# Queries and keys turned as float32 rows, and split behind PSUM: one core of a Trainium2 chip

## The chip, the cores and the metric

The kernel runs on one core of one Trainium2 chip. A core has TensorE (matrix products and transpositions, into PSUM), VectorE, ScalarE and GpSimd for elementwise work, and queues for transfers from HBM. The metric is the time of one execution on the device in microseconds (us), less is better. In the rows PE is TensorE's matmul, PEld its weight load, DVE VectorE, ACT ScalarE, POOL GpSimd.

## The reference

One layer of a decoder with 256 tokens and 1024 channels: two attention mixers in parallel, merged by sigmoid gates, then an MLP with squared ReLU. Cut to what matters:

```python
h = _rmsnorm(x, norm1_g[i])
proj = h @ w_in[i]
...
q_a = _rope(_rmsnorm(q_a.reshape(B, S, NSA_HEADS, dh), q_norm_a[i]), pos).reshape(B, S, G, R, dh)
k_s = _rope(_rmsnorm(k_s.reshape(B, S, G, dh), k_norm_slc[i]), pos)
k_w = _rope(_rmsnorm(k_w.reshape(B, S, G, dh), k_norm_win[i]), pos)
y_a = _nsa_mixer(q_a, k_c, v_c, k_s, v_s, k_w, v_w, g_nsa, ...)
q_b = _rope(_rmsnorm(q_b.reshape(B, S, DIL_HEADS, dh), q_norm_b[i]), pos)
k_b = _rope(_rmsnorm(k_b.reshape(B, S, DIL_HEADS, dh), k_norm_b[i]), pos)
y_b = _dilated_mixer(q_b, k_b, v_b)
mixed = jax.nn.sigmoid(g_ma) * (y_a @ w_o_a[i]) + jax.nn.sigmoid(g_mb) * (y_b @ w_o_b[i])
```

The first mixer (NSA) has 12 query heads of 64 in 3 key groups, over selected, window and compressed keys; the second (dilated) has 12 query and 12 key heads. Scores are sums of q times k over the 64 channels of a head.

## The kernel before

Products carry float32 as two float32r parts, hi = float32r(x) and lo = x - hi, and three passes (hi hi, hi lo, lo hi). Weights stream from HBM in pieces of 128x768. Of each piece ScalarE makes hi (L180), and VectorE, for some pieces GpSimd, makes lo (L183), five to eight pieces ahead of their use.

Projections (`proj`, L294 to L296) give rows: 128 tokens on the partitions, up to 420 columns, in two token tiles (t = 0, 1). In order: compressed keys and values, selected and window keys and values (3 key heads each), queries of the first mixer in two halves of 6 heads (qa0, qa1) beside the compression MLP, the first gates (L744 to L746), then for each half of the second mixer queries (dq), keys (dk) and values, 6 heads each; then the other gates and the first output projection.

Behind each projection a task works on the rows. `normrope` squares and sums per head, takes the power -0.5 on GpSimd (L315), rotates with the tables (L321 on GpSimd, L324 and L327 on VectorE) in the tile t1 (two buffers), and multiplies by the norm in place (L329). Then:

- queries (`q_out`): ScalarE copies the rows into hi (L342), VectorE makes lo = v - hi (L343), each head as 128 columns [hi, lo]. Six float32r transpositions (L335, in `turn`, three to a PSUM bank) give per head hi on partitions 0 to 63 and lo on 64 to 127; ScalarE casts three heads at a time out of PSUM (L336).
- keys (`k_out`): each head is written twice, as [hi, hi] (L353) and as [lo, lo] (L354), then transposed as two tiles (L335) and cast by ScalarE (L336). A score is then two products of a query tile, with [hi; hi] and with [lo; lo] (L552 for the first mixer, L693 for the second).
- the 48 compressed keys likewise (L457 to L469).

There are 8 query tiles (6 heads), 4 key tiles of 3 heads and 4 of 6 heads. The split rows lie in tiles with the tag "qk", four buffers. The attention tasks (`nsa`, `dil`) wait for the events that these tasks set; their probabilities are transposed as float32 (L511), cast to hi by ScalarE out of PSUM (L515), and lo is made by VectorE from PSUM (L516; for the compressed keys L644, L645).

The order of the program is made by `Order`: products are emitted in sequence, and steps of the tasks are set in between when a clock of estimated TensorE time says that they are due (`yield D["rope"]` leaves 8 us of it between the rows and their transposition, D["turn"] 0.3 us). A scheduler below orders the instructions of each engine by their priority and their estimated times. Each engine runs its queue in order. PSUM has 4 banks for accumulators and 6 for all else, transpositions among it.

## Time and profile before

| | us |
|---|---|
| median of 3 runs | 474.08 |
| lowest and highest | 473.75, 474.11 |
| span of the profiled execution | 474.4 |
| busy in it: TensorE, VectorE, ScalarE, GpSimd | 452.3, 351.9, 295.0, 209.0 |

The page gives each engine's busy time and its share of the span, the span in 40 slices, the chain of work that ended last, and the costliest groups of instructions. Matmuls are pipelined, so one's record is longer than the time that it takes from the next one: for that the chain of waits is read, whose pieces do not overlap.

### The profile page before, as it was taken

Reading aid. Unit: us, or ns where it says so; the run is one execution under the profiler, and the core shown is the slowest. Engines: PE = TensorE matmul, PEld = TensorE weight load, DVE = VectorE, ACT = ScalarE, POOL = GpSimd, SP = SyncE. Lnnn points to the kernel's source line nnn. Section 1 sums busy time; section 2 is a strip of 40 time slices with the busy share of each in tenths; the row PEclk is TensorE's granted clock in tenths of the full one; section 3 lists DMA queues with packets and bytes.
Section 4 is the critical chain, followed back from the end, with each engine's and each line's share of the span. In section 5 each row is a group of like instructions: output and inputs, shape, how many; then the busy total and the mean of one; then the engine's idle time right before and its main releaser. Section 6 shows DMA issues by size and latency. Waiting matters only on the chain.

```text
span 474.4 us, 9304 instructions
## 1 busy us (share of the span) xinstructions
PE 452.3 (95%) x3472; PEld 436.4 (92%) x3474; DVE 351.9 (74%) x572; ACT 295.0 (62%) x637; POOL 209.0 (44%) x203
## 2 busy tenths in 40 slices
PE   7997897999899999999999899999999999999996
PEld 6896777999798898989999899999999999999996
DVE  3959998989988999998557979956556555555450
ACT  5747678487867897858697454665656643433430
POOL 2797775779587782813043519523333310000000
PEclk8999899999899999999999999999999999999999
DMA  7973557563343144234336574777666767767720
GB/s 246 356 232 101 161 170 249 152 193 101 99 140 129 34 134 134 77 103 123 102 96 188 182 225 133 205 199 194 180 192 178 195 194 203 193 205 197 196 87 11
DMA packets 29630, 76.93 MB, mean 162 GB/s; under 512 B 3809, under 2 KB 5265, under 8 KB 29457
## 3 DMA queue, kind: packets, MB, share of 16 engines
q1 hardware_dynamic: 29584, 76.34, 54.5%
q8 instruction: 27, 0.44, 0.4%
q14 instruction: 19, 0.15, 0.1%
HBM read 75.28 MB, written 1.05 MB: 161 GB/s over the span
## 4 chain that ended last, share of the span: by engine, by line
PE 79%; DVE 10%; issue 4%; DMA 3%; ACT 2%; SPq 1%; POOL 0%; DVEq 0%; ACTq 0%; POOLq 0%
PE acc L745 18%; PE acc L746 18%; PE acc L744 18%; PE acc L295 4%; PE acc L296 4%; PE acc L294 4%; DVE wl L183 3%; PE tp L511 2%; DMA raw<-in_kv_c 2%; DMA gr<-in_gr 2%; PE tp L335 1%; PE dsp L693 1%; PE sp L552 1%; DVE t L329 1%; DVE h L873 1%
## 5 line engine op out<-in xcount | busy, mean ns | idle before, releaser
L183 DVE TENSOR_TENSOR wl<-raw,wh 128x768 fp32r<-128x768 f32 (+2 forms) x154 | 160.7, 1047 | 70.5 <-ACT wh L180 69.8
L180 ACT CAST wh<-raw 128x768 fp32r<-128x768 f32 (+2 forms) x183 | 152.1, 841 | 77.8 <-PE acc L745 66.2
L183 POOL TENSOR_TENSOR wl<-raw,wh 128x768 fp32r<-128x768 f32 (+1 forms) x29 | 56.2, 1937 | 62.5 <-ACT wh L180 35.8
L745 PE MATMUL acc<-h,wh 128*128 128x256 f32 x256 | 71.8, 281 | 0.7 <-DVE h L873 0.6
L745 PE MATMUL acc<-u,wh 128*128 128x256 f32 x256 | 71.6, 280 | 0.0
L746 PE MATMUL acc<-u,wl 128*128 128x256 f32 x256 | 71.6, 280 | 0.0
L744 PE MATMUL acc<-u,wh 128*128 128x256 f32 x256 | 71.6, 279 | 0.0
L746 PE MATMUL acc<-h,wl 128*128 128x256 f32 x256 | 71.3, 279 | 0.0
L744 PE MATMUL acc<-h,wh 128*128 128x256 f32 x256 | 71.3, 280 | 0.0
L295 PE MATMUL acc<-wl,hT 128*128 128x384 f32 (+1 forms) x176 | 63.0, 358 | 5.3 <-POOL wl L183 3.2
L294 PE MATMUL acc<-wh,hT 128*128 128x384 f32 (+1 forms) x176 | 60.3, 355 | 2.7 <-ACT wh L180 2.6
L296 PE MATMUL acc<-wh,hT 128*128 128x384 f32 (+1 forms) x176 | 61.1, 350 | 0.0
L911 POOL TENSOR_TENSOR r<-r 128x256 f32<-128x256 f32 x32 | 31.7, 992 | 54.1 <-ACT r L910 54.1
L745 PEld LDWEIGHTS acc<-h,wh 128*128 128x128 f32 x256 | 48.2, 188 | 1.2 <-DVE h L873 1.1
L746 PEld LDWEIGHTS acc<-u,wl 128*128 128x128 f32 x256 | 48.2, 188 | 0.0
L745 PEld LDWEIGHTS acc<-u,wh 128*128 128x128 f32 x256 | 48.2, 188 | 0.0
L744 PEld LDWEIGHTS acc<-u,wh 128*128 128x128 f32 x256 | 48.2, 188 | 0.0
L746 PEld LDWEIGHTS acc<-h,wl 128*128 128x128 f32 x256 | 48.1, 188 | 0.0
L744 PEld LDWEIGHTS acc<-h,wh 128*128 128x128 f32 x256 | 48.0, 188 | 0.0
L295 PEld LDWEIGHTS acc<-wl,hT 128*128 128x128 f32 x176 | 34.7, 197 | 7.3 <-POOL wl L183 3.7
L294 PEld LDWEIGHTS acc<-wh,hT 128*128 128x128 f32 x176 | 33.6, 194 | 4.1 <-ACT wh L180 3.5
L746 PE MATMUL acc<-hT,wl 128*128 128x256 f32 x128 | 37.0, 289 | 0.0
(195 smaller groups left out, 1094.7 us busy)
## 6 DMA issues: line engine op xcount, KB each, us to landing
raw<-in_cells SPq DMA_DIRECT2D x128, 384.0 KB, 3.4
raw<-in_cw SPq DMA_DIRECT2D x10, 384.0 KB, 3.7
raw<-in_q_a SPq DMA_DIRECT2D x8, 384.0 KB, 3.2
raw<-in_q_b SPq DMA_DIRECT2D x8, 384.0 KB, 3.6
raw<-in_k_b SPq DMA_DIRECT2D x8, 384.0 KB, 3.1
raw<-in_v_b SPq DMA_DIRECT2D x8, 384.0 KB, 3.2
raw<-in_kv_w SPq DMA_DIRECT2D x4, 420.0 KB, 8.3
raw<-in_kv_c SPq DMA_DIRECT2D x4, 384.0 KB, 7.0
```

What stands on the lines that cost most here:

```text
L180: nc.scalar.copy(hi[:, :m], src)
L183: eng.tensor_sub(lo[:, :m], src, f(hi[:, :m]))
L294: nc.tensor.matmul(o, hT[0][:, k, ts], hi[:, c], start=k == 0, stop=False)
L295: nc.tensor.matmul(o, hT[0][:, k, ts], lo[:, c], start=False, stop=False)
L296: nc.tensor.matmul(o, hT[1][:, k, ts], hi[:, c], start=False, stop=k == 7)
L329: nc.vector.tensor_mul(v, v, st[:, 1, :h][:, :, None].to_broadcast([128, h, 64]))
L335: nc.tensor.transpose(pt[:, i * 128:(i + 1) * 128], src[:, i].rearrange("p a d -> p (a d)"), idr)
L511: nc.tensor.transpose(pt[0:rows, i * 128:(i + 1) * 128], s, ident)
L744: nc.tensor.matmul(o, hi, a[0][k], start=start, stop=False)
L745: nc.tensor.matmul(o, hi, a[1][k], start=False, stop=False)
L746: nc.tensor.matmul(o, lo, a[0][k], start=False, stop=stop)
L911: nc.gpsimd.tensor_mul(r, r, r)
```

## The change

A query tile is transposed unsplit: v is float32, two heads of 64 side by side are the 128 columns of one transposition, three for six heads. As it leaves PSUM, ScalarE writes hi and VectorE lo, once for the heads on partitions 0 to 63 and once for those on 64 to 127; lo goes to the other half of the partitions, so that half of the heads are now stacked [hi; lo] and half [lo; hi]. Of a key tile L329 writes each head twice (768 columns for 6 heads); three heads are transposed as float32 at a time, ScalarE writes [hi; hi] and VectorE [lo; lo] from the same bank. The compressed keys likewise, with one transposition for two. `normrope` writes its last product into tiles of their own, "vq" and "vk", three buffers each, in place of t1; "qk" is gone, and so is the float32r identity `idr`. Shortened, the rest of the diff is removed comments:

```diff
-     "rbufs": 5, "wbufs": 5, "xb": 3, "phib": 4, "Pb": 4, "yb": 4, "sqb": 2, "t2b": 1, "t1b": 2, "qkb": 4,
+     "rbufs": 5, "wbufs": 5, "xb": 3, "phib": 4, "Pb": 4, "yb": 4, "sqb": 2, "t2b": 1, "t1b": 2, "vkb": 3, "vqb": 3,
...
-    idr = const.tile([128, 128], F32R, name="idr")
-        nc.vector.tensor_copy(idr, ident)
...
-        nc.vector.tensor_mul(v, v, st[:, 1, :h][:, :, None].to_broadcast([128, h, 64]))
-        return v
-
-    def turn(dst, src, m):
-        pt = tp_bank(F32R)
-        for i in range(m):
-            nc.tensor.transpose(pt[:, i * 128:(i + 1) * 128], src[:, i].rearrange("p a d -> p (a d)"), idr)
-        nc.scalar.copy(dst, f(pt[:, :m * 128]).rearrange("p (h c) -> p h c", c=128))
-        pe(m * 0.11)
+        if twice:
+            o = tok.tile([128, 6, 2, 64], F32, name="vk", tag="vk", bufs=D["vkb"])[:, :h]
+            nc.vector.tensor_mul(o, v[:, :, None, :].to_broadcast([128, h, 2, 64]),
+                                 st[:, 1, :h][:, :, None, None].to_broadcast([128, h, 2, 64]))
+        else:
+            o = tok.tile([128, 6, 64], F32, name="vq", tag="vq", bufs=D["vqb"])
+            nc.vector.tensor_mul(o, v, st[:, 1, :h][:, :, None].to_broadcast([128, h, 64]))
+        return o
 
     def q_out(v, t, qd):
-        ql = tok.tile([128, 6, 2, 64], F32R, name="ql", tag="qk", bufs=D["qkb"])
-        nc.scalar.copy(ql[:, :, 0], v)
-        nc.vector.tensor_sub(ql[:, :, 1], v, f(ql[:, :, 0]))
         yield D["rope"]
-        for a in range(0, 6, 3):
-            turn(qd[:, a:a + 3, t * 128:(t + 1) * 128], ql[:, a:a + 3], 3)
+        pt = tp_bank()
+        for i in range(3):
+            nc.tensor.transpose(pt[:, i * 128:(i + 1) * 128], v[:, 2 * i:2 * i + 2].rearrange("p a d -> p (a d)"), ident)
+        pe(0.35)
+        for b in range(2):
+            a, o = (slice(b * 64, b * 64 + 64), slice(64 - b * 64, 128 - b * 64))
+            src = pt[a, :384].rearrange("p (h c) -> p h c", c=128)
+            ts = slice(t * 128, (t + 1) * 128)
+            nc.scalar.copy(qd[a, b:6:2, ts], src)
+            nc.vector.tensor_sub(qd[o, b:6:2, ts], src, f(qd[a, b:6:2, ts]))
+        yield D["turn"]
+
+    def k_out(v, h, dst):
+        yield D["rope"]
+        for a in range(0, h, 3):
+            pt = tp_bank()
+            for i in range(3):
+                nc.tensor.transpose(pt[:, i * 128:(i + 1) * 128],
+                                    v[:, a + i].rearrange("p a d -> p (a d)"), ident)
+            pe(0.35)
+            src = pt[:, :384].rearrange("p (h c) -> p h c", c=128)
+            hi, lo = dst(0, a), dst(1, a)
+            nc.scalar.copy(hi, src)
+            nc.vector.tensor_sub(lo, src, f(hi))
             yield D["turn"]
-
-    def k_out(v, h, dst):
-        kd = [tok.tile([128, 6, 2, 64], F32R, name=f"kd{i}", tag="qk", bufs=D["qkb"]) for i in range(2)]
-        vb = v[:, :, None, :].to_broadcast([128, h, 2, 64])
-        nc.scalar.copy(kd[0][:, :h], vb)
-        nc.vector.tensor_sub(kd[1][:, :h], vb, f(kd[0][:, :h]))
-        yield D["rope"]
-        for i in range(2):
-            for a in range(0, h, 3):
-                turn(dst(i, a), kd[i][:, a:a + 3], 3)
-                yield D["turn"]
...
-            v = normrope(y[:, 0:192], 3, kind, t, 0.125, EPS)
+            v = normrope(y[:, 0:192], 3, kind, t, 0.125, EPS, twice=True)
...
-            v = normrope(y[:, 0:384], 6, 4, t, 0.125, EPS)
+            v = normrope(y[:, 0:384], 6, 4, t, 0.125, EPS, twice=True)
```

## Rows read from the trace of the kernel before

**Rows 1.** The page, its first part: busy us, share of the span, instructions.
```profile
PE 452.3 (95%) x3472; PEld 436.4 (92%) x3474; DVE 351.9 (74%) x572; ACT 295.0 (62%) x637; POOL 209.0 (44%) x203
```

**Rows 2.** Busy time by stretch: engines (instructions), granted clock, DMA share, GB/s.
```profile
38.00:77.00 39.00, 30.66 (x189) 26.99 (x188) 38.74 (x62) 26.72 (x57) 27.16 (x25) 0.96 0.57 169
77.00:108.00 31.00, 31.00 (x217) 30.07 (x217) 27.49 (x53) 22.83 (x63) 22.04 (x22) 1.00 0.59 180
108.00:126.00 18.00, 15.84 (x109) 14.20 (x106) 17.87 (x36) 12.99 (x36) 14.81 (x13) 1.00 0.41 117
126.00:195.00 69.00, 68.58 (x468) 63.16 (x467) 62.91 (x122) 56.20 (x171) 45.34 (x47) 0.98 0.35 108
195.00:202.00 7.00, 6.02 (x53) 5.73 (x52) 7.00 (x10) 6.19 (x13) 6.50 (x6) 1.00 0.35 92
202.00:264.00 62.00, 60.51 (x515) 58.90 (x517) 47.44 (x89) 43.36 (x93) 17.53 (x12) 1.00 0.44 135
```

**Rows 3.** Groups of instructions: count, busy us, mean ns, idle before.
```profile
L511 PE MATMUL tp<-ident,P 128*128 128x128 f32 x108 | 17.5, 275 | 0.0
...
L335 PE MATMUL tp<-idr,kd 128*128 128x128 f32 x72 | 9.1, 251 | 0.5 <-ACT kd L353 0.5
...
L335 PE MATMUL tp<-idr,ql 128*128 128x128 f32 x48 | 5.4, 250 | 0.0
```

**Rows 4.** The chain of waits near 200 us: start, us on the chain, what.
```profile
193.57 0.21 PE tp L335 x3
193.78 0.19 PE acc L745
193.96 0.12 PE acc L746
...
195.37 0.98 DVE t L324
...
203.51 0.44 PE tp L511 x4
```

**Rows 5.** The same chain at 214 us.
```profile
213.85 0.96 PE tp L335 x12
```

**Rows 6.** Single lines: count, least/median/greatest ns, first and last start in us.
```profile
L354 DVE TENSOR_TENSOR kd<-t,kd x8: 543/947/2180, 51.8 to 218.8; 128x384 fp32r<-128x384 f32 x4, 128x768 fp32r<-128x768 f32 x4
...
L329 DVE TENSOR_TENSOR t<-t,st x16: 341/600/2200, 49.5 to 204.7; 128x384 f32<-128x384 f32 x12, 128x192 f32<-128x192 f32 x4
...
L183 DVE TENSOR_TENSOR wl<-raw,wh x154: 939/958/2736, 6.7 to 460.9; 128x768 fp32r<-128x768 f32 x151, 128x840 fp32r<-128x840 f32 x2, 128x512 fp32r<-128x512 f32 x1
...
L342 ACT CAST ql<-t x8: 513/516/554, 66.5 to 196.4; 128x384 fp32r<-128x384 f32 x8
...
L294 PE MATMUL acc<-wh,hT x176: 332/337/522, 6.7 to 166.5; 128*128 128x384 f32 x160, 128*128 128x420 f32 x16
```

**Rows 7.** Groups by form, ScalarE: count, busy us, mean ns, idle before.
```profile
L336 ACT CAST dk<-tp 128x384 fp32r<-128x384 f32 x16 | 7.4, 485 | 3.4 <-PE tp L335 3.3
```

**Rows 8.** Groups by form, VectorE.
```profile
L516 DVE TENSOR_TENSOR plo<-tp,phi 128x384 fp32r<-128x384 f32 x12 | 6.2, 548 | 3.4 <-ACT phi L515 3.4
...
L343 DVE TENSOR_TENSOR ql<-t,ql 128x384 fp32r<-128x384 f32 x8 | 4.8, 596 | 0.0
L354 DVE TENSOR_TENSOR kd<-t,kd 128x768 fp32r<-128x768 f32 x4 | 4.6, 1154 | 0.0
...
L645 DVE TENSOR_TENSOR pc<-tp,pc 16x512 fp32r<-16x512 f32 x6 | 4.1, 680 | 0.2
...
L354 DVE TENSOR_TENSOR kd<-t,kd 128x384 fp32r<-128x384 f32 x4 | 3.8, 962 | 0.0
```

**Rows 9.** The chain of waits from 106 to 126 us.
```profile
117.17 0.55 DVE ql L343
...
124.49 0.69 DVE pc L645
```

**Rows 10.** TensorE in order of time: start, us, what, idle before.
```profile
125.23 0.49 PE L649 MATMUL pvo<-pc,vC 48*128 48x512 f32 x1 [2.16 <-DVE pc L645]
```

More of the change, by code (lines that the diff above doesn't have):

```diff
@@ L304, in proj, with normrope @@
                 yield 0
-    def normrope(y, h, kind, t, sumscale, eps):
+    def normrope(y, h, kind, t, sumscale, eps, twice=False):
         n = h * 64
@@ L456, in cmp_post @@
             nc.vector.tensor_add(t1[:, 0], t1[:, 0], t1[:, 1])
-            nc.vector.tensor_scalar(t1[:, 0], t1[:, 0], st[:, 1:2], None, op0=OP.mult)
-            kd = [tok.tile([48, 2, 64], F32R, name=f"kcd{j}", tag=f"kcd{j}", bufs=1) for j in range(2)]
-            vb = t1[:, 0][:, None, :].to_broadcast([48, 2, 64])
-            nc.scalar.copy(kd[0], vb)
-            nc.vector.tensor_sub(kd[1], vb, f(kd[0]))
-            yield D["ck"]
-            pt = tp_bank(F32R)
-            for j in range(2):
-                nc.tensor.transpose(pt[:, j * 48:(j + 1) * 48], kd[j].rearrange("p a d -> p (a d)"), idr[0:48, 0:48])
-            pe(0.2)
-            for j in range(2):
-                nc.scalar.copy(st_["kT"][j][:, :, 384:400],
-                               f(pt[:, j * 48:(j + 1) * 48]).rearrange("p (g c) -> p g c", g=3))
+            kd = tok.tile([48, 2, 64], F32, name="kcd", tag="kcd", bufs=1)
+            nc.vector.tensor_scalar(kd, t1[:, 0][:, None, :].to_broadcast([48, 2, 64]), st[:, 1:2], None, op0=OP.mult)
+            yield D["ck"]
+            pt = tp_bank()
+            nc.tensor.transpose(pt[:, 0:48], kd.rearrange("p a d -> p (a d)"), ident[0:48, 0:48])
+            pe(0.1)
+            src = pt[:, 0:48].rearrange("p (g c) -> p g c", g=3)
+            hi, lo = [st_["kT"][j][:, :, 384:400] for j in range(2)]
+            nc.scalar.copy(hi, src)
+            nc.vector.tensor_sub(lo, src, f(hi))
         else:
```

## The prediction

> **What bounds the kernel now.** I read the page first, then busy time by stretch, then the chain of waits inside each stretch, then single lines. The page says TensorE is busy 452.3 of 474.4 us [rows 1]; a matmul's record is longer than its share of the stream, so that is no proof. The stretches are [rows 2]. From 38 to 77 us VectorE is busy 38.74 of 39.00 us and TensorE only 30.66: VectorE sets the pace. From 77 to 108 TensorE is busy without a hole and VectorE has 3.5 us to spare. From 108 to 126 VectorE is full again (17.87 of 18.00), and TensorE has 2.16 us of idle time. From 126 to 195 TensorE leads (68.58 of 69.00), VectorE has 6.1 us free. From 195 to 202 VectorE is full (7.00 of 7.00) and TensorE loses 1 us. After 202 TensorE leads, VectorE has 14.6 us free up to 264. The last transposition that the change touches lies near 230 us, so all that follows 264 is unmoved. So one microsecond off TensorE counts from 77 to 108 and from 126 on; one microsecond on VectorE counts in 38 to 77, 108 to 126 and 195 to 202.
>
> **TensorE.** Before, a query tile takes 6 float32r transpositions and a key tile of three heads 6 (of six heads 12): 72 for keys and 48 for queries (8 query tiles of 6) [rows 3]. After, each six become three, in float32; the compressed keys go from two small ones to one and are left out of the sum. What float32 costs is seen in lines that stay: the probabilities at L511 are transposed in float32 with the same identity, 108 records for 108 transpositions [rows 3], and a run of four takes 0.44 us on the chain, 0.11 each [rows 4]. A float32r one takes 0.080 (twelve in 0.96) [rows 5]; a run of three takes 0.21, and the matmul behind it 0.19 in place of 0.12, so 0.28 for three, 0.093 each [rows 4]. Six old ones cost 0.48 to 0.56 us, three new ones 0.33: 0.15 to 0.23 us saved per six. There are 20 sixes; the four of the first keys run in the VectorE-bound stretch, 16 behind 77 us. 16 x 0.15 to 0.23 is 2.4 to 3.7 us; I take 2.9.
> [...]
>
> **ScalarE.** Per query tile: one copy of 0.516 goes [rows 6]; two casts out of PSUM stay two (half the partitions, same columns, 0.485 [rows 7]). Per key tile of three heads a cast of about 0.52 and one PSUM cast go; of six heads a cast of 768 columns (at most 2 x 0.516) and two PSUM casts. 8 x 0.52 + 4 x 1.0 + 4 x 2.0 = at most 16 us less, some 15, spread from 50 to 230. ScalarE is nowhere full [rows 2], so this is worth only what sits in a chain; it is not counted but as cover below.
>
> **VectorE.** Removed: 8 subtractions of queries (mean 0.596), 4 of three-head keys (0.962), 4 of six-head keys (1.154) [rows 8]: 4.8 + 3.8 + 4.6 = 13.2 us. Added: two subtractions from PSUM per query tile, one per three-head and two per six-head key tile: 16 + 4 + 8 = 28. The nearest row is L516 with 128x384 from PSUM, 0.548 [rows 8]; a half-height one is no cheaper, since L645 takes 0.680 with 16 partitions for 512 columns [rows 8]. 28 x 0.548 = 15.3 us. The multiplication L329 writes keys twice: 384 in place of 192 columns (0.54 for 0.34, the least of L354 and L329 [rows 6]), and 768 in place of 384 (0.94, the least of L183, for 0.54 [rows 6]): 4 x 0.20 + 4 x 0.40 = 2.4. Net +4.5 us, the one large price of the change. By stretch:
> 38 to 77: gone are the three-head L354 (3.8) and two L343 (1.2); new are 0.8 of wider multiplications and four subtractions (2.2). Net -2.0. Of this 1.6 is one L354 that took 2.180 where 0.543 is the least [rows 6]; whatever held it may hold another instruction. Bounds -2.0 and -0.4, and as the pace is VectorE's, the time follows. I take 0.8 us saved.
> 77 to 108: four new subtractions (2.2) of the first queries, less two old ones: +1.0 within 3.5 us of idle time. Nothing, as long as no product waits for them (first rival).
> 108 to 126: four new ones (2.2) and two wider multiplications (0.8), less two L343 (1.2): +1.8 on a full engine. On this chain lie L343 (0.55) and, before a 2.16 us hole of TensorE, the subtraction L645 (0.69) [rows 9, 10]. ScalarE's relief shortens the same chain by the two query copies of 0.52 that lie in it (L342 [rows 6]). Bounds: +1.8 and -1.0; I take their sum, 0.8 us lost.
> 126 to 264: eight query and eight key subtractions (8.8) and 0.8 of wider multiplication against the four six-head L354 (4.6) and two L343 (1.2): +3.8 in 20 us of idle time. Nothing by itself, and one thing better. The rotated rows now leave the t1 tile (2 buffers) at L329, where before they held it until the split had been made. The last projection product is at 166.5, yet L329 runs until 204.7 and the query split until 196.4 [rows 6]: the last key tiles' rotation comes as a burst (L324 at 195.37 [rows 4]) that fills VectorE from 195 to 202. With 3 buffers for queries and 3 for doubled keys it can start earlier. Worth 0 to 1.0 us (the TensorE time lost there [rows 2]); I take 0.6.
>
> Why L354 took 0.543 once and 2.180 another time is told by no row. [...]
>
> **Sum.** -2.9 -0.8 +0.8 -0.6 = -3.5 us. The profiled span is 474.4, the median 474.08 with runs from 473.75 to 474.11, so span and median are taken as one: 474.1 - 3.5 = **470.6 us**. About 0.2%, 0.95 us, is what a measurement of this kernel can tell from no change.
>
> **Rivals.**
> First, slower: the low part becomes a wait of TensorE. Before, both parts were made some 8 us of TensorE work ahead of the transpositions, and behind them only a cast stood. Now the low part is made behind transposition and cast, in VectorE's queue, and the scores' products L552 and L693 are issued soon after in TensorE's queue, with the projections behind them. If VectorE runs late there, TensorE stands still. And where VectorE is early it waits for the cast, with the weights' low parts (L183) behind it that TensorE needs: before its 12 like subtractions L516 it idled 3.4 us [rows 8], 0.28 each, so between nothing and 7.8 us for 28; nothing is taken, since such idling needs VectorE ahead of TensorE, where it has time. [...] Against: the scheduler has projections to put in between, and PSUM subtractions are steady in time. Chance of two, or of one with a loss beside it, 0.22: 475.1 to 478, near 477.
> Second, no change: the +4.5 us of VectorE eat what TensorE saves, because the stretches hand the delay on; or one stall does: 474.1 +- 0.9. Against it are the 20 us of idle VectorE behind 126. Chance 0.16.
> [...] Chance 0.14.
>
> **How the numbers follow.** Forecast 0.48 (469 to 473, 5.1 to 1.1 us saved), third rival 0.14, no change 0.16, slower 0.22. Faster by over 0.2% is 0.48 + 0.14 = 0.62, same 0.16, slower 0.22. The range leaves out about the lower half of the third case and the upper half of the slower one: 467.0 to 477.0.
>
> **What would show it.** The transpositions: 61 records fewer of L335's kind, runs of three at 0.33 us. ScalarE some 15 us less busy in all, VectorE 2 to 5 us more, its PSUM subtractions near 0.55. VectorE less than full from 195 to 202. The prediction is wrong if TensorE has holes ahead of L552 or L693 that end on the new subtractions, if a float32 transposition of queries or keys takes well over 0.11, or if a third half-clock stretch shows between 60 and 230 us.

## The result, and the profile after

The changed kernel takes 477.92 us (median of 4 runs, 477.84 to 478.09) against 473.91 us for the kernel before in the same comparison: a ratio of 1.0077 with a 95% interval of 1.0062 to 1.0092. It is slower by 0.8%: 4.0 us by these medians, 3.7 by the ratio. The forecast was 470.6 and its range ended at 477.0; the time lies above it. The profiled execution has a span of 476.2 us. A second profile of the kernel before (before_again, below) has a span of 473.0 and a time of 474.8; in all profiles of this study whose time is on record, the time is 1.7 to 2.2 us above the span. Spans are compared with that 473.0 from here on, so 3.1 us are to be explained.

TensorE's work came out much as it was costed. VectorE's total did too, but by other instructions than those of the sum (below, in the part on the prediction). The first part of the page of the changed kernel, as [rows 1]:

```profile
PE 448.9 (94%) x3411; PEld 431.3 (91%) x3413; DVE 356.9 (75%) x583; ACT 283.9 (60%) x607; POOL 209.1 (44%) x203
```

There are 61 matmul records fewer, VectorE is 5.0 us busier than in [rows 1], ScalarE 11.1 us less busy. Groups by form (count, busy us, mean ns, idle before): the new transpositions, the new subtractions, the last rotation products and ScalarE's casts of queries:

```profile
L357 PE MATMUL tp<-ident,vk 128*128 128x128 f32 x36 | 5.8, 278 | 0.5 <-DVE vk L329 0.4
L341 PE MATMUL tp<-ident,vq 128*128 128x128 f32 x24 | 4.0, 278 | 0.0
...
L348 DVE TENSOR_TENSOR qa<-tp,qa 64x384 fp32r<-64x384 f32 x8 | 4.4, 555 | 0.2
L348 DVE TENSOR_TENSOR dq<-tp,dq 64x384 fp32r<-64x384 f32 x8 | 4.4, 554 | 0.2
L363 DVE TENSOR_TENSOR dk<-tp,dk 128x384 fp32r<-128x384 f32 x8 | 4.3, 544 | 0.0
...
L329 DVE TENSOR_TENSOR vk<-t,st 128x768 f32<-128x768 f32 x4 | 3.8, 956 | 0.1
L329 DVE TENSOR_TENSOR vk<-t,st 128x384 f32<-128x384 f32 x4 | 3.8, 943 | 0.0
...
L347 ACT CAST qa<-tp 64x384 fp32r<-64x384 f32 x8 | 3.7, 469 | 4.5 <-DVE qa L348 4.5
```

A matmul's record (278 ns) is longer than its share of the stream. Taken from the start of each to the start of the next, with idle time left out, all transpositions that the change touches cost 10.6 us in before_again (122 of them) and 6.3 us after (61), so 4.3 us are saved: 0.087 us for a float32r one, 0.10 for a float32 one. The 28 subtractions from PSUM keep to 0.52 to 0.56 us.

So TensorE has 4.3 us less to do and the kernel is 3.1 us longer: 7.4 us went elsewhere. Some 6 of them are idle time of TensorE. Its holes of over 150 ns add up to 21.9 us after and 16.0 in before_again; behind 77 us they are 12.4 and 6.0. The other 1.3 us or so lie between the starts of products that stayed, without a hole that the profile tells. What released TensorE, from 77 to 264 us (us in total, times, longest): first after, then before_again.

```profile
PE pvo L527 <- DVE plo L518: 3.7, 3, 1.6
PE sp L554 <- DVE qa L348: 1.4, 1, 1.4
PE acc L292 <- DVE st L312: 1.3, 1, 1.3
PE tp L643 <- ACT P L578: 1.1, 1, 1.1
PE acc L746 <- ACT yT L547: 1.1, 1, 1.1
PE sp L554 <- ACT P L578: 1.0, 1, 1.0
...
```

```profile
PE pvo L649 <- DVE pc L645: 2.2, 1, 2.2
PE acc L744 <- ACT mT L867: 1.5, 1, 1.5
PE pvo L525 <- DVE plo L516: 1.4, 2, 1.0
...
```

Only one hole, 1.4 us, ends on a new subtraction (the queries' L348). The hole of 2.2 us in front of L649 [rows 10] is gone, and so is the stretch behind it, from 127 to 130 us, in which the granted clock of the kernel before was 0.50: from 126 to 195 us the clock is 1.00 where it was 0.98 [rows 2]. In its place stand several holes that end on old steps of the first mixer's attention: low parts of probabilities (L518, L516 before), exponentials (L578). Busy time by stretch, as [rows 2]:

```profile
77.00:108.00 31.00, 29.64 (x195) 28.58 (x194) 30.21 (x56) 21.25 (x56) 23.74 (x19) 1.00 0.60 186
108.00:126.00 18.00, 15.03 (x102) 12.80 (x100) 16.89 (x27) 12.16 (x31) 11.82 (x13) 1.00 0.28 77
126.00:195.00 69.00, 63.16 (x423) 56.32 (x422) 62.63 (x124) 50.04 (x151) 42.60 (x46) 1.00 0.38 118
195.00:202.00 7.00, 7.00 (x57) 6.31 (x56) 6.60 (x14) 6.25 (x23) 3.41 (x3) 1.00 0.20 60
```

From 126 to 195 TensorE is now busy 63.16 of 69 us, where it was busy 68.58 [rows 2]. VectorE is no busier there (62.63 for 62.91) and has 6 us to spare in both: its idle time was there and did not help. The attention's steps come late. Each of the six steps of the first mixer ends with a product of the compressed keys (L649 before, L651 after): duration, first and last start, in before_again and after.

```profile
L649 PE MATMUL pvo<-pc,vC x6: 491/495/498, 123.7 to 208.1; 48*128 48x512 f32 x6
```

```profile
L651 PE MATMUL pvo<-pc,vC x6: 492/494/498, 130.1 to 217.0; 48*128 48x512 f32 x6
```

They start 6.3 to 10.4 us later, while the projection products from 118 to 142 us are some 0.5 to 3.4 us ahead of before_again. This lateness is not a loss by itself. In cmp_old, one of the runs below, the first of them is still later (10.6 us) and the last 6.2 us late, and the span of that profile is 472.9, as short as before_again's (by all its runs it is 0.28% above the kernel before):

```profile
L657 PE MATMUL pvo<-pc,vC x6: 492/498/502, 134.3 to 214.3; 48*128 48x512 f32 x6
```

VectorE from 121 us on, in order of time, shows one way in which a step comes late (start, us, what):

```profile
121.01 2.06 DVE L325 TENSOR_TENSOR t<-t,t 128x384 f32<-128x384 f32 x1
123.00 0.94 DVE L183 TENSOR_TENSOR wl<-raw,wh 128x768 fp32r<-128x768 f32 x1
123.97 0.56 DVE L348 TENSOR_TENSOR qa<-tp,qa 64x384 fp32r<-64x384 f32 x1
```

```profile
124.58 0.52 PE L554 MATMUL sp<-kT,qa 128*128 128x272 f32 x2 [1.37 <-DVE qa L348]
```

A rotation of the second mixer's keys (L325, 2.06 us; the like step in before_again, L327 at 119.4 us, took 0.54) and a weight stand ahead of the queries' low part, and TensorE waits 1.37 us for that (the second fence). In before_again the last low parts of the first mixer's queries (L343) were made from SBUF at 91.7 and 93.5 us, some 30 us earlier, and no rotation could come between them and the scores.

### The profile page after: what moved, and what is told of

Its sections match the earlier page's. It is cut to its first block, busy times and chain, and to the rows that moved or that the text cites. A ratio compares the mean times of both kernels' runs of the same rounds, so it can differ in the third digit from the quotient of the medians.

```text
span 476.2 us, 9168 instructions
## 1 busy us (share of the span) xinstructions
PE 448.9 (94%) x3411; PEld 431.3 (91%) x3413; DVE 356.9 (75%) x583; ACT 283.9 (60%) x607; POOL 209.1 (44%) x203
## 4 chain that ended last, share of the span: by engine, by line
PE 63%; DVE 18%; issue 7%; POOL 5%; ACT 4%; DMA 1%; SPq 0%; DVEq 0%; ACTq 0%; POOLq 0%
PE acc L747 18%; PE acc L748 17%; PE acc L746 17%; DVE wl L183 4%; DVE t L325 2%; PE tp L513 2%; ACT wh L180 2%; POOL t L319 2%; POOL ropeg L268 1%; PE dsp L695 1%; DVE nm L582 1%; DVE vk L329 1%; PE acc L293 1%; DMA xT<-in_xT 1%; DVE st L311 1%
## 5 line engine op out<-in xcount | busy, mean ns | idle before, releaser
L183 DVE TENSOR_TENSOR wl<-raw,wh 128x768 fp32r<-128x768 f32 (+2 forms) x154 | 165.2, 1077 | 62.7 <-ACT wh L180 62.3
L183 POOL TENSOR_TENSOR wl<-raw,wh 128x768 fp32r<-128x768 f32 (+1 forms) x29 | 58.7, 2026 | 43.2 <-ACT wh L180 33.9
L293 PE MATMUL acc<-wl,hT 128*128 128x384 f32 (+1 forms) x176 | 61.8, 351 | 6.9 <-DVE wl L183 4.2
L292 PE MATMUL acc<-wh,hT 128*128 128x384 f32 (+1 forms) x176 | 59.0, 351 | 2.9 <-ACT wh L180 1.6
L294 PE MATMUL acc<-wh,hT 128*128 128x384 f32 (+1 forms) x176 | 60.6, 345 | 0.0
L747 PE MATMUL acc<-hT,wh 128*128 128x256 f32 x128 | 37.2, 292 | 0.0
L292 PEld LDWEIGHTS acc<-wh,hT 128*128 128x128 f32 x176 | 33.5, 194 | 4.0 <-ACT wh L180 2.2
```

Of the source, the lines that this page charges most:

```text
L183: eng.tensor_sub(lo[:, :m], src, f(hi[:, :m]))
L292: nc.tensor.matmul(o, hT[0][:, k, ts], hi[:, c], start=k == 0, stop=False)
L293: nc.tensor.matmul(o, hT[0][:, k, ts], lo[:, c], start=False, stop=False)
L294: nc.tensor.matmul(o, hT[1][:, k, ts], hi[:, c], start=False, stop=k == 7)
L747: nc.tensor.matmul(o, hi, a[1][k], start=False, stop=False)
```

## The experiments

Five theories stand in the expectations. A: ScalarE's second cast of a query tile waits for VectorE's first subtraction without need. B: VectorE's load delays the attention. C: the scores wait for low parts that are now made late. D: rotated rows, no longer held by their tile, go ahead of attention steps in VectorE's queue. E: the scheduler sets all queues anew when the work changes, and the new order costs. A ratio is always to the kernel before, run on the same chip.

**The parts alone.** casts_first is the changed kernel with the two casts of a query tile ahead of its two subtractions:

```diff
-        for b in range(2):
-            nc.scalar.copy(qd[a, b:6:2, ts], src)
-            nc.vector.tensor_sub(qd[o, b:6:2, ts], src, f(qd[a, b:6:2, ts]))
+        for b, (a, o) in enumerate(half):
+            nc.scalar.copy(qd[a, b:6:2, ts], src[b])
+        for b, (a, o) in enumerate(half):
+            nc.vector.tensor_sub(qd[o, b:6:2, ts], src[b], f(qd[a, b:6:2, ts]))
```

> The changed kernel, with the two casts of a query tile issued before its two subtractions (in the changed kernel: cast, subtraction, cast, subtraction). Theory A, a false wait: ScalarE's second cast waits for VectorE's first subtraction, with all of ScalarE's queue behind it (idle 1.76, 2.73 and 2.46 us before three of them in the changed kernel's trace); without that wait the attention steps come earlier, and most of the loss goes: 472 to 475.5 us, no idle time of ScalarE before the second cast that ends on the first subtraction. Theory B, VectorE's load: the same instructions remain on a full engine, so 477 to 478.5, as the changed kernel. Theory C, late low parts: the scores still wait for the subtractions behind VectorE's queue; 476 to 478.

Measured: 477.38 us, 1.0051 [1.0038, 1.0064]. ScalarE's waits for L348 (4.5 and 2.5 us in all) are gone, holes of TensorE 20.0 us in place of 21.9. So the wait is real. Its price is at most a small part of the loss: the time lies where B and C had it and not in A's 472 to 475.5, and the step from 1.0077 to 1.0051 is a quarter of a per cent, with intervals that overlap.

keys_only takes the old `q_out` back (with `turn`, `idr` and "qk"); queries_only takes the old `k_out` and the old compressed keys back, so the keys stay in t1 and "qk":

```diff
 # keys_only
-            o = tok.tile([128, 6, 64], F32, name="vq", tag="vq", bufs=D["vqb"])
+            nc.vector.tensor_mul(v, v, st[:, 1, :h][:, :, None].to_broadcast([128, h, 64]))
...
+        for a in range(0, 6, 3):
+            turn(qd[:, a:a + 3, t * 128:(t + 1) * 128], ql[:, a:a + 3], 3)
 # queries_only
+        for i in range(2):
+            for a in range(0, h, 3):
+                turn(dst(i, a), kd[i][:, a:a + 3], 3)
```

> Only the keys are changed; queries are split, transposed as float32r and cast as before. TensorE loses 36 of the 61 transpositions' worth (12 sixes, about 2.4 us), ScalarE about 11 us of work, VectorE's load moves by under 1 us. Theory A (the false wait is in the query half alone): 470.5 to 472.5 us. Theory B (load of VectorE, of which queries bring some 4 us): 471 to 473. Theory C (late low parts, in keys as well as queries): 474 to 476.5, with TensorE idle before the scores' products on the keys' subtraction.

> Only the queries are changed; keys are split, transposed and cast as before. Theories A and B: the loss is here, 476 to 479.5 us, and ScalarE idles on the first subtraction as in the changed kernel. Theory C (as much in the keys): 474 to 476.

Measured: 480.37 us, 1.0119 [1.0096, 1.0143], and 483.40 us, 1.0184 [1.0169, 1.0200]. Both lie above all that was expected, and either half costs more than the whole (1.0077). No sum of prices of the two parts can give this. In queries_only 3.7 us are one hole before the compression's products, waiting for a weight's low part near 72 us, while the first query is cast out of PSUM at 79.0. before_again is the kernel before, as a second profile:

> The kernel before itself, for a second profile: the first one's span of 474.4 us is longer than the spans of 472.2 to 473.8 us of its later runs, which lie 1.8 us under their times. Expected: span 472 to 474, time 1.8 above it, and TensorE's idle time behind 77 us no more than in the first profile (some 5 us), so that lines of it can be set beside the changed kernel's.

**Buffers.** own_tile is the kernel before with the last rotation product in a tile of its own, three buffers; t1_four is the kernel before with four buffers of t1. Neither adds or takes away work.

```diff
 # own_tile
-        nc.vector.tensor_mul(v, v, st[:, 1, :h][:, :, None].to_broadcast([128, h, 64]))
+        o = tok.tile([128, 6, 64], F32, name="vo", tag="vo", bufs=3)[:, :h]
+        nc.vector.tensor_mul(o, v, st[:, 1, :h][:, :, None].to_broadcast([128, h, 64]))
 # t1_four
-"t1b": 2
+"t1b": 4
```

> The kernel before, with the last product of the rotation written to a tile of its own (three buffers) in place of the tile that it rotates in; nothing else. The prediction's term of 0 to 1.0 us: 473.0 to 474.0 if freeing the rotating tile early lets the burst from 195 to 202 us go, VectorE then not full there. If the order of the attention steps is what counts, 474 plus or minus 1 either way, and the burst stays since the split rows' four buffers hold it.

> The kernel before with four buffers in place of two for the tile t1 that the rows are rotated in; no instruction is added or removed. Theory D, rows that run ahead: the buffers held back the rotations of the last projections (second dilated queries and keys), and once they are free earlier the scheduler puts those rotations before attention steps in VectorE's and GpSimd's queues, the attention steps come late, and TensorE has holes from 140 to 175 us. D: 476.5 to 479 us, 2 to 4 above the kernel before, both multiplications of the last keys before 180 us. If the place of these rotations is without effect (theories A to C): within 0.7 us of the kernel before.

Measured: 477.91 us, 1.0061 [1.0048, 1.0075], and 479.47 us, 1.0098 [1.0080, 1.0117]. Both are slower with the same work, and by more than was expected (474 plus or minus 1, and 476.5 to 479). In own_tile the last rotation product of the second half's keys stands at 158.8 us in the first token tile, where it stood at 197.9 in before_again (in the second tile 195.6 for 203.3), which is what D says, and TensorE has new holes. But t1_four has fewer holes than the kernel before (14.2 us), and a lower granted clock. Its stretches from 38 and from 126 us:

```profile
38.00:77.00 39.00, 32.77 (x186) 30.10 (x186) 36.94 (x62) 25.19 (x55) 25.71 (x25) 0.82 0.53 163
...
126.00:195.00 69.00, 66.56 (x437) 60.36 (x435) 59.25 (x119) 53.95 (x159) 45.08 (x46) 0.95 0.37 109
```

The granted clock is 0.82 for 39 us and 0.95 for 69. What a lower clock costs TensorE is seen in the kernel before: 128x384 products start 0.17 to 0.18 us apart near 126.5 us, at a granted clock of 1.00, and 0.32 apart from 127 to 130 us, at 0.50.

```profile
126.31 0.34 PE L295 MATMUL acc<-wl,hT 128*128 128x384 f32 x1
126.48 0.34 PE L296 MATMUL acc<-wh,hT 128*128 128x384 f32 x1
126.66 0.36 PE L294 MATMUL acc<-wh,hT 128*128 128x384 f32 x1
...
127.46 0.52 PE L294 MATMUL acc<-wh,hT 128*128 128x384 f32 x1
127.78 0.52 PE L295 MATMUL acc<-wl,hT 128*128 128x384 f32 x1
128.10 0.52 PE L296 MATMUL acc<-wh,hT 128*128 128x384 f32 x1
```

So, here and below, the time lost to the clock is estimated as half of the time at 0.50: for t1_four some 7.0 and 3.5 us (by the means: 0.18 x 39 and 0.05 x 69), against some 1.6 and 1.4 in [rows 2]. By this estimate t1_four loses by the clock. D alone does not explain both.

dk_two is the changed kernel with the doubled six-head keys in a tag of their own with two buffers, so that they run ahead less; dk_two_casts_first has the casts of casts_first as well:

```diff
-            o = tok.tile([128, 6, 2, 64], F32, name="vk", tag="vk", bufs=D["vkb"])[:, :h]
+            o = tok.tile([128, 6, 2, 64], F32, name="vk", tag="vk" if h == 3 else "vk6", bufs=D["vkb"] if h == 3 else 2)[:, :h]
```

> The changed kernel with a tile tag of its own, of two buffers, for the doubled keys of six heads (before it, three shared with the keys of three heads): the second dilated keys wait until the first are transposed, and their rotations come near 200 us as in the kernel before. Theory D: 1.5 to 3 us less than the changed kernel (ratio to the kernel before 1.001 to 1.005). Theories A to C: as the changed kernel, ratio 1.006 to 1.009.

> Both: two buffers for the doubled keys of six heads, and the two casts of a query tile before its two subtractions. Theories A and D together: the saving of TensorE (some 4 us on its stream) is left; ratio to the kernel before 0.993 to 1.001. Theory B (VectorE's load): 1.004 to 1.008.

Measured: 481.14 us, 1.0137 [1.0122, 1.0152], and 475.58 us, 1.0018 [1.0010, 1.0027]. No theory expected the first; the second lies just above what A and D together gave (0.993 to 1.001). The two are told apart in the program only by where the casts stand, and differ by 1.2% (0.3% of it is the slower pace of the last section); in casts_first the same edit gave 0.26%. Such edits do not add up like terms.

**Load and delay.** extra_subs is the kernel before with eight subtractions that nobody uses, in place in the second PSUM bank of each query tile (4.3 us of VectorE):

```diff
+        return pt
...
-            turn(qd[:, a:a + 3, t * 128:(t + 1) * 128], ql[:, a:a + 3], 3)
+            pt = turn(qd[:, a:a + 3, t * 128:(t + 1) * 128], ql[:, a:a + 3], 3)
+            if a:
+                src = f(pt[:, :384]).rearrange("p (h c) -> p h c", c=128)
+                nc.vector.tensor_sub(src, src, f(qd[:, a:a + 3, t * 128:(t + 1) * 128]))
```

> The kernel before with one subtraction more behind every query tile, from its second PSUM bank of transposed heads and in place there (its result is used by nothing): 8 subtractions of 128x384, some 4.4 us of VectorE, the net load that the change adds, and no score waits for them. Theory B (VectorE's load alone): ratio to the kernel before 1.004 to 1.009. Theories A and C (it is waits, not load): within 0.997 to 1.003.

Measured: 483.54 us, 1.0193 [1.0175, 1.0210]: 9 us for 4.3 us of an engine that idled 20 us behind 126 [rows 2]. It is twice what theory B expected. In its profile 13.7 us run at a granted clock of 0.50, in before_again 6.8 (means over the spans 0.986 and 0.993), so some 3.4 of the 9 us are the clock by the same estimate; the order tells of the rest (below).

The other three start from dk_two_casts_first. late_scores leaves more time between a split and the scores; cmp_old takes the old compressed keys back; rope5 turns the rows 3 us of emission time earlier:

```diff
 # late_scores (and a delay behind the compressed keys)
-"rope": 8, "turn": 0.3
+"rope": 8, "turn": 2.5
 # rope5
-"rope": 8
+"rope": 5
```

> The kernel of dk_two_casts_first (ratio 1.0018) with the delay between a transposition and the event that lets the scores go raised from 0.3 to 2.5 us of TensorE's estimated time, and the same delay behind the compressed keys. Theory C (scores wait for low parts just made): the holes of TensorE before the scores that end on the new subtractions (1.72 us on the compressed keys' and 0.46 on a query's in dk_two_casts_first) go, ratio 0.994 to 1.000. If the lateness of the attention steps as such is what costs: 1.002 to 1.008.

> The kernel of dk_two_casts_first with the compressed keys split before their transposition, as in the kernel before. Theory C: the hole of 1.72 us before the first scores goes, 0.5 to 2 us less, ratio 0.997 to 1.001. If that hole is only filled by another: 1.001 to 1.003.

> The kernel of dk_two_casts_first with 5 in place of 8 us of TensorE's estimated time between the rows and their transposition, since one product and not a cast and a subtraction more stands between them now. Theory C: transpositions and low parts come earlier against the scores, holes that end on the new subtractions shrink: ratio 0.996 to 1.001. If TensorE then waits for the rows at the transpositions: 1.002 to 1.008, with holes before the transpositions that end on the rotation's last product.

Measured: late_scores 480.45 us, 1.0127 [1.0109, 1.0145]; cmp_old 476.34, 1.0028 [1.0010, 1.0045]; rope5 475.97, 1.0028 [1.0016, 1.0041]. More time for the low parts, the cure by theory C, makes it worse, more than either theory said. The hole of 1.72 us that C named is gone, the query's 0.5 stays, and 17.1 us run at a granted clock of 0.50 where dk_two_casts_first has 6.8 (means 0.981 and 0.993): half of the difference is 5.1 of the 5.3 us between the two spans. In cmp_old the hole is filled by another, of 3.1 us, that ends on an old step of VectorE (the compressed values); in rope5 it grew from 1.7 to 2.4. So no cure of C gained anything; that late low parts cost nothing is not shown by this.

**The order held.** The scheduler orders each engine's queue by priority and estimated times, so an edit moves instructions that it does not touch. Take the matmuls of two traces by tile and shape, and count the fewest that must be moved to make one queue out of the other: of those shared with before_again 254 of 3350 in the changed kernel, 172 of 3472 in own_tile, 231 in t1_four, 251 in extra_subs; of VectorE's, 101 of 537 in the changed kernel. (The counts in the expectations are of the program, instruction by instruction, and are higher.) For the next runs the instructions of one engine that two kernels share were chained in a listed order by edges that say only "issue after" (shortened):

```python
for row in ORDER:      # one list of instruction numbers for each engine
    for a, b in zip(row, row[1:]):
        tc.add_manual_dep(by[f"I-{b}"], f"I-{a}", ISSUE_ORDER_ONLY)
```

In the traces of the runs held in the old order not one shared matmul stands elsewhere. own_in_order and extra_in_order are own_tile and extra_subs in the order of the kernel before:

> The kernel before with the last rotation product in a tile of its own, as in own_tile, held in the order of the kernel before on all four engines. own_tile took 0.61% longer with the same work; 330 of 3499 TensorE instructions stood elsewhere. Theory E: as before, 474 to 475.2. If the tile itself costs (by its place in SBUF or by its buffers): 477 to 478.5 again.

> The kernel before with the eight unused PSUM subtractions of 128x384 behind the query tiles (about 4.4 us of VectorE), as in extra_subs, but with the instructions of TensorE, VectorE, ScalarE and GpSimd held in the order of the kernel before; only the eight subtractions find their own place in VectorE's queue. In extra_subs the scheduler had set 448 of 3499 TensorE instructions and 97 of 574 of VectorE elsewhere. Theory E (a new order of the queues is what costs, not the work): within 2 us of the kernel before, 473.5 to 476.5. Theory B (VectorE's load itself delays the attention): at least half of the 9 us stays, 479 to 484.

Measured: own_in_order 475.38 us, 1.0018 [1.0001, 1.0034], for 1.0061 in its own order; extra_in_order 478.73 us, 1.0078 [1.0049, 1.0107], for 1.0193, between what E and B expected. So the chaining itself costs 0.3% at the most, and some 1.3 of the 2 us by which own_tile is slower than own_in_order are the pace of the last section. The eight subtractions are the same, so the larger part of extra_subs is order. The six attention products, in extra_subs and extra_in_order:

```profile
L653 PE MATMUL pvo<-pc,vC x6: 492/498/500, 124.6 to 218.5; 48*128 48x512 f32 x6
```

```profile
L653 PE MATMUL pvo<-pc,vC x6: 492/498/502, 126.7 to 211.9; 48*128 48x512 f32 x6
```

extra_subs begins 0.9 us late and ends 10.4 us late; held in order the delay is 3.0 us at the first and 3.8 at the last, of which 0.7 stand there already at 55 us and 1.7 are half of a 3.4 us stretch at a granted clock of 0.50 near 77 us (mean 0.94 from 77 to 108 us). So 4.3 us of added work on VectorE cost some 0.6 us by waiting at the first and 1.4 at the last, and with the clock in all 0.8%, whose interval is wide: B holds, for the smaller part.

after_in_order is the whole change in the order of the kernel before; cf_in_order the same with both casts ahead:

> The whole change, with the instructions that both kernels share held in the order of the kernel before on all four engines (a query or key tile's three transpositions stand where the first three of the old ones stood, its last rotation product where the old one stood); the new subtractions find their own place in VectorE's queue. For this the emission clock counts the old transposition times. Theory E: TensorE's 4.3 us come through, less what new waits take: 470 to 473. Theory B: VectorE's load costs as in the change as it was: 476 to 480. Theory D (rotated rows that run ahead) is shut off here too: by it alone 470 to 474, but then own_in_order below must gain as well.

> As after_in_order, with both casts of a query tile set ahead of its two subtractions, so that ScalarE's second cast does not wait for VectorE. Theory E: 470 to 472, and if the false wait (theory A) counts, 1 to 2.5 us below after_in_order. Theory B: 475 to 478.

Measured: 481.50 us, 1.0141 [1.0122, 1.0160], and 479.66 us, 1.0109 [1.0089, 1.0129]. E expected 470 to 473 and 470 to 472: it fell here, and both lie above B's ranges too. The old order is worse for the change than the new one, and the trace shows where. ScalarE, VectorE, TensorE, and the stretch, of after_in_order:

```profile
116.38 0.47 ACT L347 CAST qa<-tp 64x384 fp32r<-64x384 f32 x1 [6.90 <-DVE qa L348]
```

```profile
116.89 0.56 DVE L348 TENSOR_TENSOR qa<-tp,qa 64x384 fp32r<-64x384 f32 x1 [0.34 <-ACT qa L347]
```

```profile
117.59 1.09 PE L518 MATMUL tp<-ident,P 128*128 128x128 f32 x4 [4.25 <-DVE qa L348]
```

```profile
108.00:126.00 18.00, 13.75 (x75) 12.97 (x74) 16.68 (x32) 8.69 (x26) 12.11 (x10) 0.81 0.42 115
```

ScalarE's second cast waits 6.90 us for VectorE's first subtraction, which stands in its queue behind two weights' low parts, two last rotation products and a rotation of 1.83 us. The second subtraction follows the cast, and TensorE's next transposition, of probabilities, starts only when that one has ended: 4.25 us are lost. It reads nothing that the subtraction writes; what it most likely waits for is the query tile's PSUM bank, which the subtraction is the last to read (argued from the program, not tested). The granted clock is at 0.50 for 6.8 of the 18 us (mean 0.81), from 116.8 us on, 3.5 us into this hole. That is a stall by a late low part, as in the first rival, but on another path than the rival's: no score waits here. With both casts ahead (cf_in_order) this hole is gone; the largest left up to 264 us are 1.9 and 1.5 (L524, low parts of probabilities), 1.0 (the compressed ones') and 0.9 us (the compressed keys' new low part). TensorE's queues of the two runs are alike but for one record, so here the casts alone are worth 0.3%, with intervals that overlap. Set beside before_again product by product, after_in_order is 0.7 us ahead at 76 us, 0.9 behind at 107, 3.9 at 131 and 6.2 from 260 us on: about half of its loss arises at this stall.

before_new_order is the mirror: rows and splits of the kernel before, TensorE and ScalarE in the order of the changed kernel, VectorE and GpSimd left free:

> The mirror of after_in_order: the rows and splits of the kernel before, with TensorE and ScalarE held in the order of the changed kernel for the instructions that both share (the old steps that the change removes, and VectorE and GpSimd, find their own place). 348 of TensorE's and 68 of ScalarE's instructions stand elsewhere than in the kernel before. No low part is made behind a transposition here, so none of the new waits can arise. If the new order is itself a price (theory E), 477 to 481: slower than the kernel before although the work is its own. If the loss of the change lies in its new chain alone (transposition, cast, low part, scores), the order costs nothing here: 474 to 475.5.

Measured: 480.31 us, 1.0117 [1.0094, 1.0140]. In the trace none of TensorE's and ScalarE's instructions that it shares with the changed kernel stands elsewhere than there, and 30 of VectorE's 537 do. The old work, with none of the new waits possible, is slower in the new order, and its attention is as late as the changed kernel's:

```profile
L650 PE MATMUL pvo<-pc,vC x6: 491/497/500, 130.4 to 218.2; 48*128 48x512 f32 x6
```

So the new order has a price of its own, though not all of this is shown to be order: of the 6.9 us between its profiled span (479.9) and before_again's, 1.1 lie behind 320 us, in the pace of the last section. Another 1.7 are half of the 3.4 us that it runs longer at a granted clock of 0.50 (mean 0.91 from 38 to 77 us, 0.96 in before_again). The four cases, as ratios to the kernel before (in the second column, the order of TensorE and ScalarE):

| | order of the kernel before | order of the changed kernel |
|---|---|---|
| rows and splits before | 1 (own_in_order 1.0018) | 1.0117 |
| rows and splits changed | 1.0141 | 1.0077 |

dk_two_old_clock is dk_two_casts_first with the emission clock counting the old transposition times, so that all tasks' steps are emitted as in the kernel before, and the scheduler is free:

```diff
-        pe(0.35)
+        pe(0.33)
...
         yield D["turn"]
+        pe(0.33)
+        yield D["turn"]
```

> dk_two_casts_first (475.58 us, 1.0018) with the emission clock counting the transposition times of the kernel before (0.66 us a query tile and a three-head key tile, 1.32 a six-head one), so that the steps of all tasks are emitted in the order of the kernel before, and the scheduler is left free. If the shorter clock of the change is part of the loss, 472 to 474.5; if it is not, 475 to 477; if every new order costs as in own_tile and t1_four, 476 to 480.

Measured: 475.16 us, 1.0010 [0.9999, 1.0022], between what two theories said: as fast as the kernel before, within 0.2%. Of its matmuls 198 stand elsewhere than in before_again, more than in own_tile: a new order is not dear by the number of moves. No version of the study beats the kernel before.

## Why the prediction was wrong

**TensorE, 2.9 us saved: right for the work, and too small.** 4.3 us came off its stream [rows 3 to 5], and the kernel kept none of it. Six float32r ones cost 0.52 and three float32 ones 0.31, a saving of 0.21, inside the 0.15 to 0.23 used; on the 16 sixes of the sum that is 3.4, and the trace saves on all 20. Each float32 transposition of queries and keys is one record of 0.272 us at the median, 0.10 of the stream.

**ScalarE, some 15 us: 11.1 by the page.** The page counts time in which records overlap once; the durations of the casts that the change touches add up to 16.3 us less. It was not counted, and bought nothing that shows. What was missed is the new wait of the second cast. It needs nothing from the first subtraction: they read different partitions of one bank, and write different columns of the same partitions of the query tile. Which of the two made it wait, no run tells; with the casts first (casts_first) ScalarE's waits for L348, 4.5 and 2.5 us in all, are gone.

**VectorE, +4.5 us: +5.0 by the page, and that is luck.** The removed subtractions were 13.2 us, as said, and the new ones 15.3 (0.544 to 0.555 each, by group, for 0.548). But the last rotation products, counted at +2.4, came to -1.3: the sum took them at their least time, and they took 16.6 us before and 15.3 after. So the instructions that the change touches add 0.8 us and not 4.5. The rest are others that take longer, the rotations above all, [rows 6] by form, before and after:

```profile
L329 DVE TENSOR_TENSOR t<-t,st 128x384 f32<-128x384 f32 x12 | 14.6, 1217 | 0.6 <-POOL st L315 0.6
...
L327 DVE TENSOR_TENSOR t<-t,t 128x384 f32<-128x384 f32 x12 | 9.7, 805 | 0.2
...
L329 DVE TENSOR_TENSOR t<-t,st 128x192 f32<-128x192 f32 x4 | 2.0, 499 | 0.0
```

```profile
L325 DVE TENSOR_TENSOR t<-t,t 128x384 f32<-128x384 f32 x12 | 16.0, 1335 | 1.8 <-POOL t L319 1.7
L333 DVE TENSOR_TENSOR vq<-t,st 128x384 f32<-128x384 f32 x8 | 7.7, 978 | 0.0
```

The rotations' sum (L327, now L325) took 6.3 us more, the weights' low parts 4.5 more, the rotations' first product 3.4 less. For 384 columns L325, with two inputs in SBUF, took between 0.54 and 2.20 us, and L348, with one input in PSUM, between 0.54 and 0.56. The rows are in the last section.

**38 to 77 us, 0.8 saved: not settled.** VectorE is busy 0.85 us less there than in before_again (36.50 for 37.35), inside the bounds of 0.4 to 2.0. The 80th projection product of L294 (L292 after), at 77 us, is 1.4 us earlier than in before_again, but the 70th, at 62, 1.6 later, and the 82nd, at 87, in its old place.

**77 to 108 and 126 to 264, nothing; 108 to 126, 0.8 lost: the step that failed.** It set VectorE's new work against VectorE's idle time of the stretch, put the wait at nothing, and let TensorE's 2.9 us come through. That idle time exists still, yet TensorE went from 0 to 1.4 us without work between 77 and 108 and from 0.4 to 5.8 between 126 and 195, where the sum had no more. The sum was made as if every other instruction kept its place and its wait. By before_new_order, the new places cost the old work 1.2%, 5.8 us (with the reserve on the pace made there); by after_in_order, the old places cost the new work 1.4%. No term of the sum could hold either.

**126 to 264, t1 released earlier, 0.6 gained: wrong sign.** Rows did run ahead (the last rotation, L325, starts at 162.0 us, where L327 started at 202.0 in before_again, though its last product still stands at 201.8), VectorE is no longer full from 195 to 202 (6.60 of 7.00), and TensorE does not idle there; but the kernel as a whole kept nothing of it. own_tile, this step by itself, costs 0.6%, and 0.2% in the old order, where the rows cannot run ahead; more than half of that difference is pace.

**The first rival** was the nearest, and its 475.1 to 478 holds the measured time, for the most part by luck. Its mechanism, scores that wait for a late low part, is one hole of 1.4 us in the changed kernel, and the granted clock behind it is 1.00. A late low part that does cost much, 4.25 us and an estimated 3.4 of clock (half of 6.8 us at 0.50), is in after_in_order, on another path. The word against it, that the scheduler puts projections in between, was right: it did, and attention came 6 to 10 us late, which by cmp_old is not a loss by itself. **The third rival**, more gain: the hole before L649 did close, and the granted clock behind it is 1.00 where it was 0.50, but this gain was spent with the rest. No run shows the 3.6 us for a stall together with its clock that the 467.0 of this rival and the 475.1 to 478 of the first rest on: the hole of 2.16 us before L649 [rows 10] had 3.4 us at 0.50 behind it, the 1.4 us of the changed kernel have none, and the 4.25 us of after_in_order have 6.8.

**Baseline.** Span and median were taken as one; the time lies 1.8 us above the span, and the one profiled execution shown (474.4) was 1.4 us longer than before_again. The forecast starts from the median, so neither moved it.

Open: which of the moved instructions make the new order dear; that order is the cause of the changed kernel's loss is argued from these runs, not isolated in it. before_new_order leaves VectorE and GpSimd free, so its price is that of one more order, not of the changed kernel's exactly; and that the changed work gains 0.4% over the old work in that order (1.0077 for 1.0117) is as uncertain as that. What the edit would be worth in an order made for it was not found.

## What to carry to other kernels

Where a scheduler sets the queues, a sum over added and removed work forecasts only what holds if the queues stay as they are; ask which instructions lose or gain a wait or a buffer, expect hundreds of others to move, and give that a term, measured by an edit that adds no work: here 0.6 to 1.2% in three of them, each time to the slow side. Idle time of an engine is no cover when its queue is in order and a late chain runs through it: in extra_in_order 4.3 us of added work on VectorE, idle for some 20 us behind 126 in the kernel before, cost some 0.6 to 1.4 us by waiting. A total that comes out as forecast proves nothing until its terms are set beside the trace one by one. To tell work from order, hold the order: run the change in the old order, and the old work in the new one.

## What the runs showed of the hardware

The prediction asked why one L354 took 2.180 us and another 0.543. The long one stands at 52.6 us, beside a low part of a weight (L183) on GpSimd; no other L354 of 384 columns has GpSimd work of that kind beside it. GpSimd of the kernel before, then of the changed kernel, then VectorE of the changed kernel:

```profile
52.54 1.86 POOL L183 TENSOR_TENSOR wl<-raw,wh 128x768 fp32r<-128x768 f32 x1
```

```profile
120.83 1.84 POOL L183 TENSOR_TENSOR wl<-raw,wh 128x768 fp32r<-128x768 f32 x1 [2.84 <-ACT wh L180]
...
202.03 2.40 POOL L183 TENSOR_TENSOR wl<-raw,wh 128x768 fp32r<-128x768 f32 x1 [1.97 <-ACT wh L180]
```

```profile
203.44 0.55 DVE L363 TENSOR_TENSOR dk<-tp,dk 128x384 fp32r<-128x384 f32 x1
```

In the changed kernel seven of the sixteen L325 took 1.94 to 2.20 us, and each runs beside such an L183 of GpSimd; the nine that took 0.35 to 0.56 have none beside them for more than 0.1 us. The L325 of 2.06 us that held up the queries' low part at 121.01 is one of the seven. L363, with one input in PSUM, keeps its 0.55 beside the same work.

From about 290 us on the change touches nothing, and yet a stream of 128x256 products runs at one of two paces, 345 or 342 in 40 us. before_again, then own_tile:

```profile
330.00:370.00 40.00, 40.00 (x345) 40.00 (x344) 23.91 (x34) 24.99 (x48) 13.72 (x15) 1.00 0.70 188
```

```profile
330.00:370.00 40.00, 40.00 (x342) 40.00 (x341) 23.20 (x33) 24.93 (x48) 13.51 (x15) 1.00 0.68 186
```

The granted clock is 1.00 in both. Over the stretch from 290 us to the end this is some 1.6 us, over half of own_tile's loss of 2.9; queries_only and dk_two have the slower pace too, the changed kernel the faster. keys_only goes over to the slower one near 380 us, and before_new_order lies between the two (342 to 344). What sets it was not found.
